# Activation rows of 132 words and longer weight buffers in a two-block transformer kernel

## The chip, the cores and the metric

The kernel runs on one core of one Trainium2 chip. The metric is the device time of one execution in microseconds, as the median of several runs. Engine names: PE is the matrix engine (TensorE), PEld its weight loads, DVE is VectorE, ACT is ScalarE, POOL is GpSimd, SP is SyncE, which issues the transfers.

## What is computed

A residual stream x of 256 tokens by 1024 channels goes through two layers of a first block (feed-forward, a mixer of a linear recurrence, a retention and a short convolution, feed-forward), and then one layer of a second block (two kinds of banded attention, an MLP, a gated embedding). In short:

```
for l in range(2):
    x = x + 0.5 * rmsnorm(swiglu(rmsnorm(x), ffn1_w_in[l], ffn1_w_out[l]))
    x = x + rmsnorm(hybrid_mixer(rmsnorm(x), ...))
    x = x + 0.5 * rmsnorm(swiglu(rmsnorm(x), ffn2_w_in[l], ffn2_w_out[l]))
h = x + rmsnorm(concat(windowed_attention, dilated_attention) @ w_o)
h = h + rmsnorm(relu(rmsnorm(h) @ w_up) ** 2 @ w_down)
out = h + rmsnorm(sigmoid(h @ w_ple_gate + b) * (p @ w_ple_proj))
```

All inputs are float32, and nearly all arithmetic is in products of activations with large weight matrices.

## The kernel before

**Three products for one.** A float32 product is made from three products of a rounded type (`float32r`, four bytes a word). Every activation block and every weight group is split into a rounded part and the rest: `uh`/`ul` for activations, `wh`/`wl` for weights. `mm3` (lines 164 to 171) then issues `uh*wh`, `uh*wl` and `ul*wh` into the same accumulator, on lines 165, 166 and 167. The activation is the stationary operand (128 columns, loaded into the array by a weight load of its own ahead of each matmul), the weight the moving one (512 columns, or 256 in the narrow last chunk of the feed-forward).

**Weights.** 334 groups of 128x2048 words come from memory one after the other. `load` (line 136) takes three tiles: `raw` from a pool of 3 buffers, `wh` and `wl` from a pool with 5 buffers for each name; SP issues the transfer into `raw`. `convert` (line 132) casts `raw` to `wh` on ACT and writes `raw - wh` to `wl` on DVE, in two halves of 1024 words. `grp` (line 153) hands out views of `wh` and `wl`.

**Activations.** `uh[t]` and `ul[t]` (lines 106 and 107), for the two halves t of the tokens, hold the transposed activation as 8 blocks k of 128 words, one block behind the other. They are written by `split` (line 200: a cast on ACT, a subtraction on DVE) in pieces of 4 blocks, after four transposes on PE (`tr_split`, line 235), and read by `proj` (line 270): 8 blocks by 3 products, 24 matmuls, for each 512 output columns of each half. The second kind of product, `acc_out` (line 283), takes its stationary operand from other tiles (`hl`, line 292, out of the pool `b4`, rows of 4096 bytes), four matmul triples to two blocks and two halves of 512 columns.

**Order.** The order of PE's work is that of the program. Other work is put between the triples by `later` (line 172): it counts triples, and what is due is issued by `mm3`; thus four transposes (line 209) stand between matmuls in several places.

**Where the tiles lie.** A tile takes the same range of bytes in each of the 128 partitions, and the pools follow one another: constants, `raw`, `w`, `gain`, `b4`, `b2`, small ones. The sizes are multiples of 128 bytes (`uh0` 4096, `raw` and `wh` 8192, `b4` 4096, `b2` 2048), and the small constants ahead of them are filled up with a tile `even` that nothing reads, so every operand of the `float32r` matmuls starts at a multiple of 128 bytes. Partition memory is nearly full. 16,384 bytes at its start are set aside as scratch for transfers that POOL issues; the kernel issues all its transfers from SP.

Of the kernel before, what the change touches and what calls it, by code (L numbers as in the profile page):

```python
# [12 lines left out]
F32R = mybir.dt.float32r  # L13
# [5 lines left out]
P = 128  # L19
# [53 lines left out]
def build(ctx: ExitStack, tc: tile.TileContext, a: dict, plan: list):  # L73
    nc = tc.nc
    V, A, G, T = nc.vector, nc.scalar, nc.gpsimd, nc.tensor

    def pool(name, bufs, **kw):
        return ctx.enter_context(tc.tile_pool(name=name, bufs=bufs, **kw))

    const = pool("const", 1)  # L80
    rawp = pool("raw", NRAW)
    wp = pool("w", NW)
# [20 lines left out]
    G.memset(mhalf, -0.5)  # L103
    junk = const.tile([P, D], mybir.dt.bfloat16, name="junk")
    x = [const.tile([P, D], F32, name=f"x{t}") for t in range(2)]
    uh = [const.tile([P, 8, P], F32R, name=f"uh{t}") for t in range(2)]
    ul = [const.tile([P, 8, P], F32R, name=f"ul{t}") for t in range(2)]
    cst = const.tile([P, L, 12, 8], F32, name="cst")
    cos = const.tile([P, 2, P], F32, name="cos")
    sin = const.tile([P, 2, P], F32, name="sin")  # L110
# [25 lines left out]
    def load(rec, parts):  # L136
        gi = len(plan)
        plan.append(rec)
        raw = rawp.tile([P, 2048], F32, tag="raw", name=f"raw{gi}")
        wh = wp.tile([P, 2048], F32R, tag="wh", name=f"wh{gi}")  # L140
        wl = wp.tile([P, 2048], F32R, tag="wl", name=f"wl{gi}")
        step = 2048 // parts
        for h in range(0, 2048, step):
            tail[0] = nc.sync.dma_start(raw[:, h:h + step], a["wts"][gi, :, h:h + step])
        return raw, wh, wl
# [7 lines left out]
    def grp(*rec):  # L153
        n = rec[-1]
        if rec in ready:
            raw, wh, wl = ready.pop(rec)
        else:
            raw, wh, wl = load(rec, 1)
            step = 2048 // CONV
            for h in range(0, 2048, step):  # L160
                convert(wh, wl, raw, slice(h, h + step))
        return wh.rearrange("p (k n) -> p k n", n=n), wl.rearrange("p (k n) -> p k n", n=n)
# [771 lines left out]
    for i in range(2):  # L934
        ready[recs[i]] = load(recs[i], 4 - 2 * i)
    nc.sync.dma_start(x[1], a["x"][P:, :])
    for i in range(2, 4):
        ready[recs[i]] = load(recs[i], 1)
# [75 lines left out]
def _layout(inputs):  # L1014
    d = {}
    d["x"] = inputs["x"][0]
    d["positions"] = inputs["positions"].astype(np.int32).reshape(2, P).T
    rows = np.zeros((len(GROW), D), np.float32)
    for (n, l), r in GROW.items():
        if n == "g_out_2":  # L1020
            rows[r] = np.concatenate([inputs["g_out_a_2"][0], inputs["g_out_b_2"][0]])
        else:
            rows[r] = inputs[n][l]
    d["gains"] = rows
    d["g0"] = inputs["ffn1_pre_g"][0].reshape(8, P).T

    def cols(v):
        return v.reshape(L, -1, 8, P).transpose(3, 0, 1, 2)
    d["cst"] = np.concatenate([cols(inputs[n]) for n in (
        "lru_conv_w", "lru_conv_b", "lru_b_a", "lru_b_x", "lru_lambda", "sc_conv_w")]  # L1030
        + [np.zeros((P, L, 1, 8), np.float32)], axis=2)
    w = np.stack([inputs["lru_w_a"], inputs["lru_w_x"]], axis=1).reshape(L, 2, 8, P, 64)
    d["wab"] = w.transpose(0, 3, 1, 2, 4)
    d["rel_bias_table_2"] = inputs["rel_bias_table_2"]
    d["sink_a_2"] = inputs["sink_a_2"]
    d["pT"] = inputs["p_2"][0, 0].T.reshape(2, P, S).transpose(1, 0, 2)
    d.update(_constants())
    return {k: np.ascontiguousarray(v) for k, v in d.items()}


def _weights(inputs, plan):
    w2 = inputs["w_in_2"]
    perm = np.arange(w2.shape[2])
    halves = np.arange(512).reshape(2, 4, 64).transpose(1, 0, 2).reshape(-1)
    for c in (0, 768, 1280):
        perm[c:c + 512] = c + halves
    src = dict(inputs)
    src["w_in_2"] = w2[:, :, perm]
    w = np.empty((NG, P, 2048), np.float32)
    for i, (name, l, k0, kn, c0, n) in enumerate(plan):  # L1050
        blk = src[name][l][k0 * P:(k0 + kn) * P, c0:c0 + n]
        w[i] = blk.reshape(kn, P, n).transpose(1, 0, 2).reshape(P, 2048)
    return w


def _program(inputs):
    import concourse.bacc as _bacc

    nc = _bacc.Bacc("TRN2", target_bir_lowering=False, num_devices=1)
    arrays = _layout(inputs)  # L1060
    args = {n: nc.dram_tensor(n, v.shape, mybir.dt.from_np(v.dtype), kind="ExternalInput").ap()
            for n, v in arrays.items()}
    args["wts"] = nc.dram_tensor("wts", (NG, P, 2048), F32, kind="ExternalInput").ap()
    args["out"] = nc.dram_tensor("out", (S, D), F32, kind="ExternalOutput").ap()
    plan = []
    with tile.TileContext(nc) as tc:
        build(tc, args, plan)
    arrays["wts"] = _weights(inputs, plan)
    return nc, arrays, plan
# [9 lines left out]
```

## Time and profile before

| | before |
|---|---|
| median of three runs | 2024.33 us (2023.94 to 2028.44) |
| the profiled execution, device time | 2028.99 us |
| its span, first to last instruction | 2027.2 us |
| mean granted clock of PE, share of full speed | 0.987 |
| PE busy | 1972.9 us (97%) |
| weight loads busy | 1623.8 us (80%), beside the matmuls |
| DVE busy | 1668.2 us (82%) |
| ACT busy | 1037.3 us (51%) |
| transfers, mean share of the 16 DMA engines | 50% |

The profile is of one execution. Matmuls overlap: one takes some 0.39 us from its start to its end, and the next starts before that end, so the pace of the engine is read from the distances between starts in the timeline, and not from the mean duration. A busy PE is therefore not PE at its peak. Times are read to 0.01 us, so a distance of starts is taken over several matmuls.

### The profile page before, as it was taken

The page shows a single profiled execution, that of the slowest core. Times are in us where ns is not written, and L with a number is a line of the kernel's source. Part 1 is how long each engine was busy: PE and PEld are TensorE (multiplying, and loading weights), DVE is VectorE, ACT ScalarE, POOL GpSimd, SP SyncE. Part 2 cuts the span into 40 slices and gives each one's busy share as a digit, 9 for nine tenths or more (in the row PEclk, how much of TensorE's full clock was granted, in tenths as well). Part 3 has the DMA queues.
Part 4 walks back from the last instruction along what each step waited for, and adds up shares of the span by engine and source line. Part 5 has one row for each costly group of instructions (what it writes and reads, how often), then busy time and mean ns, then how long its engine had stood idle before and what let it go on. Part 6 is the DMA issues. An engine that isn't in the chain of part 4 may idle for free.

```text
span 2027.2 us, 24429 instructions
## 1 busy us (share of the span) xinstructions
PE 1972.9 (97%) x9170; PEld 1623.8 (80%) x9170; DVE 1668.2 (82%) x2893; ACT 1037.3 (51%) x1384; POOL 58.5 (3%) x116
## 2 busy tenths in 40 slices
PE   9999999999999999999999999999999999999997
PEld 7778868788788888888887778887888888787886
DVE  7989789776877998988878995777789897679997
ACT  6444676444444543544466843454454445654553
POOL 0000000000010000000000000000010000010000
PEclk9999999999999999999999999999999999999999
DMA  6555533654445454555653546435545556424542
GB/s 250 192 208 198 187 134 137 244 189 166 166 160 212 173 207 181 198 197 187 239 190 107 183 184 220 169 115 199 205 166 208 198 207 207 161 94 149 220 183 102
DMA packets 56319, 369.72 MB, mean 182 GB/s; under 512 B 6582, under 2 KB 8886, under 8 KB 13704
## 3 DMA queue, kind: packets, MB, share of 16 engines
q1 hardware_dynamic: 56200, 368.16, 49.9%
q8 instruction: 72, 1.18, 0.2%
q14 instruction: 47, 0.39, 0.1%
HBM read 367.05 MB, written 1.08 MB: 182 GB/s over the span
## 4 chain that ended last, share of the span: by engine, by line
PE 65%; DVE 24%; ACT 4%; issue 3%; DMA 2%; POOL 0%; SPq 0%; DVEq 0%; POOLq 0%; ACTq 0%
PE c L165 13%; PE c L166 13%; PE c L167 13%; DVE ht L224 9%; DVE wl L134 8%; PE o L166 7%; PE o L167 7%; PE o L165 7%; DMA raw<-wts 2%; ACT wh L133 2%; DVE sbT L224 2%; DVE ya L224 2%; PE tp L209 2%; PE tp L456 1%; PE pv L762 1%
## 5 line engine op out<-in xcount | busy, mean ns | idle before, releaser
L134 DVE TENSOR_TENSOR wl<-raw,wh 128x1024 fp32r<-128x1024 f32 (+1 forms) x670 | 787.7, 1216 | 171.9 <-ACT wh L133 168.7
L133 ACT CAST wh<-raw 128x1024 fp32r<-128x1024 f32 (+1 forms) x670 | 670.0, 1046 | 336.4 <-PE c L167 163.6
L165 PE MATMUL c<-wh,uh 128*128 128x512 f32 (+1 forms) x1912 | 740.4, 387 | 14.4 <-DVE v L608 5.6
L166 PE MATMUL c<-wl,uh 128*128 128x512 f32 (+1 forms) x1912 | 734.9, 384 | 11.1 <-DVE wl L134 11.1
L167 PE MATMUL c<-wh,ul 128*128 128x512 f32 (+1 forms) x1912 | 734.3, 384 | 0.0
L165 PEld LDWEIGHTS c<-wh,uh 128*128 128x128 f32 x1912 | 363.2, 190 | 89.5 <-DVE v L608 6.5
L166 PEld LDWEIGHTS c<-wl,uh 128*128 128x128 f32 x1912 | 363.4, 190 | 82.5 <-DVE wl L134 12.6
L167 PEld LDWEIGHTS c<-wh,ul 128*128 128x128 f32 x1912 | 362.9, 190 | 71.1 <-issue 1.2
L224 DVE STREAM_TRANSPOSE ht<-sil 32x128 f32<-32x128 f32 (+1 forms) x768 | 223.9, 292 | 10.7
L224 DVE STREAM_TRANSPOSE ht<-sg 32x128 f32<-32x128 f32 x256 | 77.5, 303 | 3.5
L224 DVE STREAM_TRANSPOSE ht<-mh 32x128 f32<-32x128 f32 x256 | 77.5, 303 | 3.4
L195 POOL TENSOR_SCALAR ms<-ss 128x1 f32<-128x1 f32 x52 | 21.9, 421 | 1936.8 <-ACT junk L190 1915.6
L306 ACT ACTIVATE sil<-c,r 128x512 f32<-128x512 f32 (+1 forms) x48 | 31.3, 651 | 41.0 <-PE c L167 40.9
L311 DVE SCALAR_TENSOR_TENSOR sil<-c,r,sil 128x512 f32<-128x512 f32 (+1 forms) x48 | 33.7, 702 | 13.3 <-PE c L167 13.1
L224 DVE STREAM_TRANSPOSE ya<-yat 32x128 f32<-32x128 f32 x128 | 38.7, 302 | 6.0 <-ACT yat L482 4.3
L224 DVE STREAM_TRANSPOSE sbT<-sbt 32x128 f32<-32x128 f32 x128 | 38.8, 303 | 2.0
L197 POOL TENSOR_TENSOR r<-ms,mhalf 128x1 f32<-128x1 f32 x54 | 35.4, 656 | 4.5
L201 ACT CAST h2h<-ht 128x512 fp32r<-128x512 f32 x10 | 6.2, 623 | 52.2 <-DVE ht L224 52.2
L166 PE MATMUL o<-wl,h1h 128*128 128x512 f32 x80 | 31.4, 392 | 0.2 <-DVE wl L134 0.2
L166 PE MATMUL o<-wl,h4h 128*128 128x512 f32 x80 | 31.2, 390 | 0.0
L165 PE MATMUL o<-wh,h3h 128*128 128x512 f32 x80 | 31.2, 390 | 0.0
L166 PE MATMUL o<-wl,h3h 128*128 128x512 f32 x80 | 31.2, 390 | 0.0
(334 smaller groups left out, 2434.1 us busy)
## 6 DMA issues: line engine op xcount, KB each, us to landing
raw<-wts SPq DMA_DIRECT2D x332, 1024.0 KB, 4.8
tb<-row SPq DMA_DIRECT2D x8, 384.0 KB, 5.4
gain_ffn_post_g<-gains SPq DMA_DIRECT2D x4, 512.0 KB, 7.6
dec<-dec SPq DMA_DIRECT2D x4, 384.0 KB, 5.6
gain_ffn_pre_g<-gains SPq DMA_DIRECT2D x3, 512.0 KB, 8.5
x<-x SPq DMA_DIRECT2D x2, 512.0 KB, 5.7
raw<-wts SPq DMA_DIRECT2D x4, 256.0 KB, 5.5
raw<-wts SPq DMA_DIRECT2D x2, 512.0 KB, 6.4
```

The source lines that it names most:

```text
L133: A.copy(wh[:, sl], raw[:, sl])
L134: V.tensor_tensor(wl[:, sl], raw[:, sl], wh[:, sl].bitcast(F32), ALU.subtract)
L165: T.matmul(ps, xh, wh, start=first, stop=False)
L166: T.matmul(ps, xh, wl, start=False, stop=False)
L167: T.matmul(ps, xl, wh, start=False, stop=last)
L195: G.tensor_scalar(ms, ss, mul / n, mul * EPS, ALU.mult, ALU.add)
L197: G.tensor_tensor(r, ms, mhalf, ALU.pow)
L209: T.transpose(tp[:, j, :], src[:, (b + j) * P:(b + j + 1) * P], ident)
L224: V.transpose(dst[32 * j:32 * j + 32, :, 32 * q:32 * q + 32], sv[32 * q:32 * q + 32, :, 32 * j:32 * j + 32])
L306: A.activation(sil[t], ps, AF.Silu, scale=r2[t])
L311: V.scalar_tensor_tensor(sil[t], ps, r2[t], sil[t], ALU.mult, ALU.mult)
L456: T.matmul(ps[b:b + 64, j, :], wab[b:b + 64, g, 4 * c + j0 + j, :], xc[b:b + 64, j0 + j, :], start=True, stop=True)
```

## The change

The blocks of `uh` and `ul` get rows of 132 words of which 128 are used: block k starts 528 k bytes behind the tile's start. Each `wh` and `wl` buffer gets 2056 words of which 2048 are used; `wl` leaves its first 4 words free, so its data start 16 bytes into the buffer. The scratch at the start of partition memory is made smaller, 1024 bytes in place of 16,384. No instruction is added or taken away, and the order is the same.

```diff
-    uh = [const.tile([P, 8, P], F32R, name=f"uh{t}") for t in range(2)]
-    ul = [const.tile([P, 8, P], F32R, name=f"ul{t}") for t in range(2)]
+    uh = [const.tile([P, 8, P + 4], F32R, name=f"uh{t}")[:, :, :P] for t in range(2)]
+    ul = [const.tile([P, 8, P + 4], F32R, name=f"ul{t}")[:, :, :P] for t in range(2)]
...
-        wh = wp.tile([P, 2048], F32R, tag="wh", name=f"wh{gi}")
-        wl = wp.tile([P, 2048], F32R, tag="wl", name=f"wl{gi}")
+        wh = wp.tile([P, 2056], F32R, tag="wh", name=f"wh{gi}")[:, :2048]
+        wl = wp.tile([P, 2056], F32R, tag="wl", name=f"wl{gi}")[:, 4:2052]
...
-    nc = _bacc.Bacc("TRN2", target_bir_lowering=False, num_devices=1)
+    nc = _bacc.Bacc("TRN2", target_bir_lowering=False, num_devices=1, dynamic_dma_scratch_size=1024)
```

What follows for the addresses, as remainders of 128 bytes: `uh` and `ul` tiles are 4224 bytes and start at 0, so block k starts at 16 k. A weight buffer is 8224 bytes, so the five `wh` buffers start at 0, 32, 64, 96 and 0, and the data in the five `wl` buffers at 48, 80, 112, 16 and 48. The ten buffers together are 64 over a multiple of 128, so all that comes behind them (`gain`, `b4`, `b2`) starts at 64: the stationary operands of `acc_out` are all at 64.

## Rows read from the trace of the kernel before

**Rows 1.** The page, part 1: busy us, share of the span, instructions.

```profile
PE 1972.9 (97%) x9170; PEld 1623.8 (80%) x9170; DVE 1668.2 (82%) x2893; ACT 1037.3 (51%) x1384; POOL 58.5 (3%) x116
```

**Rows 2.** Groups by line and shape, PE: busy us, mean ns, idle before and releasers.

```profile
L165 PE MATMUL c<-wh,uh 128*128 128x512 f32 x1752 | 694.9, 397 | 14.4 <-DVE v L608 5.6 <-ACT sil L306 3.5 <-DVE sil L311 3.1
...
L165 PE MATMUL c<-wh,uh 128*128 128x256 f32 x160 | 45.5, 284 | 0.0
...
L165 PE MATMUL o<-wh,h3h 128*128 128x512 f32 x80 | 31.2, 390 | 0.0
```

**Rows 3.** Timeline of PE, a stretch of `acc_out`: start us, duration us, instruction.

```profile
1009.48 0.39 PE L167 MATMUL o<-wh,h3l 128*128 128x512 f32 x1
...
1010.84 0.39 PE L167 MATMUL o<-wh,h3l 128*128 128x512 f32 x1
```

**Rows 4.** Timeline of PE, matmuls of 256 columns.

```profile
999.96 0.28 PE L166 MATMUL c<-wl,uh 128*128 128x256 f32 x1
...
1001.04 0.28 PE L166 MATMUL c<-wl,uh 128*128 128x256 f32 x1
```

**Rows 5.** Timeline of PE in a stretch at the lower clock.

```profile
551.47 0.63 PE L167 MATMUL c<-wh,ul 128*128 128x512 f32 x1
...
554.03 0.63 PE L167 MATMUL c<-wh,ul 128*128 128x512 f32 x1
```

**Rows 6.** Busy us by stretch: length, engines, then granted clock, DMA share, GB/s.

```profile
551.30:554.30 3.00, 3.00 (x8) 2.34 (x8) 3.00 (x4) 2.26 (x3) 0.00 (x0) 0.50 0.82 339
```

**Rows 7.** Timeline of PE behind four transposes.

```profile
225.82 0.39 PE L165 MATMUL c<-wh,uh 128*128 128x512 f32 x1
226.05 0.39 PE L166 MATMUL c<-wl,uh 128*128 128x512 f32 x1
226.28 0.39 PE L167 MATMUL c<-wh,ul 128*128 128x512 f32 x1
226.51 0.60 PE L209 MATMUL tp<-ident,xat 128*128 128x128 f32 x4
226.86 0.48 PE L165 MATMUL c<-wh,uh 128*128 128x512 f32 x1
227.18 0.40 PE L166 MATMUL c<-wl,uh 128*128 128x512 f32 x1
227.41 0.40 PE L167 MATMUL c<-wh,ul 128*128 128x512 f32 x1
227.65 0.40 PE L165 MATMUL c<-wh,uh 128*128 128x512 f32 x1
227.88 0.39 PE L166 MATMUL c<-wl,uh 128*128 128x512 f32 x1
228.10 0.39 PE L167 MATMUL c<-wh,ul 128*128 128x512 f32 x1
...
229.26 0.39 PE L166 MATMUL c<-wl,uh 128*128 128x512 f32 x1
...
229.94 0.39 PE L166 MATMUL c<-wl,uh 128*128 128x512 f32 x1
```

**Rows 8.** What PE waited for, longest first: us, times, longest us.

```profile
PE c L166 <- DVE wl L134: 11.1, 3, 4.0
PE tp L456 <- DVE xc L448: 9.7, 6, 3.2
```

**Rows 9.** Groups of ACT by shape: the cast into `uh`, and one into longer rows.

```profile
L201 ACT CAST uh<-tp 128x512 fp32r<-128x512 f32 x32 | 17.5, 580 | 3.5 <-PE tp L209 3.2
L201 ACT CAST qkh<-tp 128x512 fp32r<-128x512 f32 x16 | 9.3, 581 | 23.3 <-PE tp L209 23.3
```

**Rows 10.** Groups of DVE by shape: the two subtractions.

```profile
L134 DVE TENSOR_TENSOR wl<-raw,wh 128x1024 fp32r<-128x1024 f32 x666 | 785.0, 1219 | 170.5 <-ACT wh L133 167.3
L202 DVE TENSOR_TENSOR ul<-tp,uh 128x512 fp32r<-128x512 f32 x32 | 21.0, 683 | 1.8 <-ACT uh L201 1.5
L202 DVE TENSOR_TENSOR qkl<-tp,qkh 128x512 fp32r<-128x512 f32 x16 | 10.9, 679 | 0.0
```

**Rows 11.** The page, part 3: queues of transfers, packets, MB, share of 16 engines.

```profile
q1 hardware_dynamic: 56200, 368.16, 49.9%
q8 instruction: 72, 1.18, 0.2%
q14 instruction: 47, 0.39, 0.1%
```

## The prediction

> **What bounds the kernel now.** I read the page first. PE is busy 97% of the span and DVE 82% [rows 1], and the waits of PE are small: the largest entry is 11.1 us, the next 9.7 us [rows 8]. So time comes or goes with the pace of PE, and the pace is read from distances between starts.
>
> In a quiet stretch six matmuls of 512 columns take 1010.84 - 1009.48 = 1.36 us, 226.7 ns each [rows 3]. Nine of 256 columns take 1.08 us, 120.0 ns each [rows 4]. At half the granted clock (0.50 [rows 6]) six of 512 columns take 2.56 us, 426.7 ns each [rows 5], which is 512 columns at 1.2 GHz and nothing else. Half of it is 213.3 ns, and that is what 512 columns would take at full clock. So at full clock each matmul pays 13.3 ns on top, and one of 256 columns pays as much (120.0 - 106.7). A cost that is the same for both widths and that vanishes where the columns go by at half the speed is not work of the array; it looks like time lost in bringing operands to it, and a weight load runs beside every matmul. That is the only place where addresses can act on the bound.
>
> How much is at stake: lines 165 to 167 have 3 x 1752 matmuls of 512 columns and 3 x 160 of 256 in the projections [rows 2]. `acc_out` and the small projection of the last block, by the loops of the code, have 840 triples, 2520 matmuls (feed-forwards 352, mixers 320, attention output and MLP 160, embedding 8 triples; one group of 80 is in [rows 2]). Together 8256, and 8256 x 13.3 ns = 110 us, 5.4% of the span. This is the most that the change could give.
>
> **Is the 13.3 ns a matter of phase?** The rows behind four transposes say yes. Before them the distance is 0.23 us. After them the first matmul comes late, and then the distances are 0.23, 0.24, 0.23, 0.22: over the nine matmuls from 227.18 to 229.26 us they make 2.08 us, 231.1 ns each, 4.4 ns over the quiet pace; over the next three, 0.68 us, 226.7 ns again [rows 7]. Nothing has changed in operands, shapes or clock within that stretch; only the time at which the matmuls start has been shifted by the transposes. So the price of a matmul depends on how its stream of words stands in time to something else, and left alone the stream falls back into one stable position, the quiet pace. Two more facts from the same rows: 226.7 and 120.0 ns are 34 and 18 times 6.67 ns, so the quiet paces lie on steps of that size; and among the unquiet distances only one is clearly under the quiet one (0.22 us), most are over it.
>
> All operands of before start at the same remainder of 128 bytes (by the sizes of the tiles), so no row shows two remainders. What they do is bounded from these neighbours.
>
> **The change part by part.**
>
> (a) *Moved operands.* The remainder of the stationary block now moves by 16 bytes from k to k, and the moving operand jumps between `wh` and `wl` at each matmul, between remainders that differ by an odd multiple of 16. If the remainder acts as a shift in time does, the stream is disturbed at each matmul and doesn't come back into the quiet position: it pays the unquiet mean, 4.4 ns more. Projections: 5256 x 4.4 = 23.1 us, and 480 x 4.4 = 2.1 us for the narrow ones. `acc_out`: its stationary operand stays at one remainder (64), but its moving operand alternates as well, 2520 x 4.4 = 11.1 us. Sum 36.3 us. The bounds of a single matmul are the shortest and the longest distance of the stretch, about 0.22 and 0.24 us, so -7 to +13 ns; times 8256 that is -58 to +107 us, and I take the mean of the stretch because the remainders run through many values rather than sit at one.
>
> (b) *Cover.* A slower PE gives DVE and ACT time, and some of PE's waits get shorter; of the 11.1 and 9.7 us [rows 8] I give back 3 us. Net +33 us.
>
> (c) *Splits into `uh` and `ul`.* 32 casts and 32 subtractions (and 4 of each at the start) now write four rows of 128 words with a gap. The nearest rows are those of `qkh` and `qkl`, which write four rows of 128 words 256 apart: 581 against 580 ns, 679 against 683 ns [rows 9, 10]. So 0; bounds of 10 ns either way on 72 instructions are under 1 us, and DVE and PE work beside them.
>
> (d) *`wl` 16 bytes into its buffer.* 666 subtractions of 1219 ns [rows 10]. Subtractions of 512 words differ by some ns between tiles (679 to 683); 13 ns either way would be 9 us of DVE, which has 18% of the span free. I take 0; if the cover were gone, at most the 11.1 us that PE waits for `wl` would grow by a few us.
>
> (e) *Smaller scratch, other base addresses.* The queues are one driven by hardware and two for instructions [rows 11], so nothing uses the scratch: 0. Transfers go into `raw`, whose remainder stays 0.
>
> The sum stands against the profiled execution, 2028.99 us with a span of 2027.2, which is 4.7 us over the median of the runs. The change is taken over to the median: 2024.3 + 33 = 2057.
>
> [...] The rows show a time beside the columns that depends on phase [rows 3 to 5, 7]. [...]
>
> **The rivals.**
>
> *Second road to slower: a line more to read.* The steps of 6.67 ns could be fetches of a piece of fixed size. A stream that starts inside a piece would need one fetch more, one step. If a piece is 64 bytes (512 columns of 4 bytes in 213.3 ns are 64 bytes in 6.67 ns), `wl` always starts inside, `wh` in two buffers of five, so of three matmuls 1 + 2 x 0.4 = 1.8 pay: 0.6 x 6.67 x 8256 = 33 us, 2057 too. Both roads end in the same place, and I count them as one case.
>
> *No change.* If the position in time comes from the instruction stream and not from the operands, remainders do nothing: 2024. For it: the quiet pace is the same whatever buffer and block is read, and whatever ACT and DVE do. Against it: those all share one remainder.
>
> *Faster: starts off the steps.* If the quiet distance is long because every operand starts at the same remainder, each matmul has to wait for the next step of 6.67 ns. With remainders that move, the start may fall anywhere between two steps, and half a step is saved on average: 3.33 x 8256 = 27.5 us, 1997. It decides from the point where the wait for the step is a larger part of the 13.3 ns than the collision with the weight load. For it: both widths lie on whole steps. Against it: behind the transposes the starts are off the steps and the distances are longer, not shorter [rows 7]. In the extreme all 13.3 ns go, 110 us, and then DVE at 1668 us of work would come near to being the bound; I'd put 1940 for that.
>
> *The change doesn't do what it says*: the views are cut from larger tiles, and the addresses follow from sizes; I see no way in which they don't move.
>
> **How the numbers follow.** Slower (unquiet mean or a line more): 0.45, between +15 us (only the projections pay, at half the price) and +45. No change: 0.22. Faster: 0.33, of which 0.22 for about half a step (1990 to 2015) and 0.11 for more. Within 0.3% (6 us) is about what a measurement of this kernel can't tell from no change; this share is nearly all of the no-change case. The predicted time is that of the likeliest case, 2057, whose own range is 2035 to 2070. The range that should hold the time reaches over the no-change case to the mild gain: 1990 to 2070, leaving out 0.10 below and 0.08 above.
>
> **What would show it.** In the changed kernel's timeline, quiet stretches of projections: if their nine-matmul distances are near 231 ns and uneven, (a) holds; if they are even and one step longer in some, the line rival; 226.7 throughout is no change; anything under 224 is the faster rival. In `acc_out` the same should be seen, with two alternating distances. The distances at half clock must stay 426.7 ns. The groups of casts and subtractions must keep their means to 10 ns. The prediction is wrong if remainders act on the collision itself and not only on its timing, since then some remainders could be free of it.

## The result, and the profile after

The change makes the kernel slower: 2043.78 us (2043.75 to 2045.03) against 2024.33, a ratio of 1.0092 with a 95% interval of 1.0069 to 1.0115, or 19.4 us. The forecast was 2057, slower, with 1990 to 2070 as its range. The direction came out, and so did the place of the cost, the pace of PE's matmuls; the reason given for it came out only in part. The size was too large by 13 us, nearly all of it in the step on cover.

The page after, part 1 (busy us, share of the span, instructions); [rows 1] answer to it:

```profile
PE 1998.2 (98%) x9170; PEld 1618.0 (79%) x9170; DVE 1669.2 (82%) x2893; ACT 1037.1 (51%) x1384; POOL 55.8 (3%) x116
```

PE has 25 us more, DVE and ACT the same. Where it comes from is seen in the timeline of PE after (start us, duration us, instruction), in a stretch of a projection and then in one of `acc_out`, which answers [rows 3]:

```profile
752.51 0.39 PE L165 MATMUL c<-wh,uh 128*128 128x512 f32 x1
752.74 0.39 PE L166 MATMUL c<-wl,uh 128*128 128x512 f32 x1
752.97 0.39 PE L167 MATMUL c<-wh,ul 128*128 128x512 f32 x1
753.20 0.40 PE L165 MATMUL c<-wh,uh 128*128 128x512 f32 x1
753.43 0.40 PE L166 MATMUL c<-wl,uh 128*128 128x512 f32 x1
753.67 0.40 PE L167 MATMUL c<-wh,ul 128*128 128x512 f32 x1
...
758.07 0.40 PE L165 MATMUL c<-wh,uh 128*128 128x512 f32 x1
```

```profile
774.78 0.39 PE L165 MATMUL o<-wh,h1h 128*128 128x512 f32 x1
...
780.36 0.39 PE L165 MATMUL o<-wh,h1h 128*128 128x512 f32 x1
```

24 distances of a projection take 5.56 us, 231.7 ns each, and 24 of `acc_out` 5.58 us, 232.5 ns, where before each took 226.7. There are no transposes in either stretch: the quiet pace of before isn't found again in them. Over the whole trace (all distances up to 242 ns between starts of 512-column matmuls outside the stretches at lower clock) the mean goes from 227.1 to 232.0 ns in the projections and from 227.0 to 232.0 in `acc_out`.

The mean granted clock (us from first to last instruction, then the clock), first before, then after:

```profile
core 0: 2027.2 us, clock 0.987
```

```profile
core 0: 2042.0 us, clock 0.994
```

PE ran at the lower of its two levels (0.50, the other is 1.00) for 52.6 us in twelve stretches before and for 24.5 us in six after, by the trace's record of the clock. The waits got shorter too: these two entries answer [rows 8] (us, times, longest us).

```profile
PE c L166 <- DVE wl L134: 8.7, 3, 3.3
PE tp L456 <- DVE xc L448: 7.8, 5, 2.7
```

### The profile page after: what moved, and what is told of

It reads as the page before. It is cut to its first block, busy times and chain, and to the rows that moved or that the text cites. A ratio compares the mean times of both kernels' runs of the same rounds, so it can differ in the third digit from the quotient of the medians.

```text
span 2042.0 us, 24429 instructions
## 1 busy us (share of the span) xinstructions
PE 1998.2 (98%) x9170; PEld 1618.0 (79%) x9170; DVE 1669.2 (82%) x2893; ACT 1037.1 (51%) x1384; POOL 55.8 (3%) x116
## 3 DMA queue, kind: packets, MB, share of 16 engines
q8 instruction: 72, 1.18, 0.2%
## 4 chain that ended last, share of the span: by engine, by line
PE 74%; DVE 18%; ACT 3%; DMA 2%; issue 2%; POOL 0%; SPq 0%; DVEq 0%; POOLq 0%; ACTq 0%
PE c L165 16%; PE c L166 16%; PE c L167 16%; PE o L165 7%; PE o L167 7%; PE o L166 7%; DVE ht L224 6%; DVE wl L134 5%; DMA raw<-wts 2%; DVE sbT L224 2%; PE tp L209 2%; DVE ya L224 2%; ACT wh L133 1%; PE tp L456 1%; PE pv L762 1%
## 5 line engine op out<-in xcount | busy, mean ns | idle before, releaser
L311 DVE SCALAR_TENSOR_TENSOR sil<-c,r,sil 128x512 f32<-128x512 f32 (+1 forms) x48 | 33.7, 702 | 14.4 <-PE c L167 14.2
L165 PE MATMUL o<-wh,h4h 128*128 128x512 f32 x80 | 31.6, 396 | 0.0
L165 PE MATMUL o<-wh,h2h 128*128 128x512 f32 x80 | 31.6, 395 | 0.0
```

The source lines that it names most:

```text
L165: T.matmul(ps, xh, wh, start=first, stop=False)
L311: V.scalar_tensor_tensor(sil[t], ps, r2[t], sil[t], ALU.mult, ALU.mult)
```

## The experiments

The changed kernel does three things at once: smaller scratch, longer rows of the stationary operand, longer buffers of the moving one. Runs 1 to 4 take them apart, runs 6 to 8, 10 and 11 go through constant differences, and runs 5, 9 and 12 settle what kind of remainder counts. All have three rounds against the kernel before on the same chip. A difference means: remainder of the stationary operand less that of the moving one, for the weight load that runs beside a matmul. Paces are distances of starts between 512-column matmuls; a mean over the trace is taken as above. Remainders and differences are worked out from the sizes of the tiles and the order of the pools.

**Theory and rivals at the start.** A: each move of a remainder disturbs the phase, and the quiet position is lost. B: a moving operand that starts inside a piece of 64 bytes costs a step. Later C, D, E as the expectations say.

**1. The scratch alone.**

```diff
-    nc = _bacc.Bacc("TRN2", target_bir_lowering=False, num_devices=1)
+    nc = _bacc.Bacc("TRN2", target_bir_lowering=False, num_devices=1, dynamic_dma_scratch_size=1024)
```

> The kernel before with the smaller scratch alone, so that all tiles move down by 15,360 bytes and every matmul operand keeps the remainder 0 of 128 bytes. Every theory of remainders: no change, 2024 us, and quiet stretches at 226.7 ns from start to start for 512 columns. If the place in memory matters by more than its remainder, or the scratch is used, something else; then the 19.4 us of the change are not those of its remainders.

Measured: ratio 1.0003 (0.9993 to 1.0012), projections 227.1 ns, `acc_out` 226.9, clock 0.986. The scratch doesn't count, and neither does moving every tile by 15,360 bytes, which keeps all remainders up to 512. All kernels below have this edit too.

**2. Longer rows of the stationary operand alone.**

```diff
-    uh = [const.tile([P, 8, P], F32R, name=f"uh{t}") for t in range(2)]
+    uh = [const.tile([P, 8, 132], F32R, name=f"uh{t}")[:, :, :P] for t in range(2)]
```

(The same for `ul`, here and in all runs below that change `uh`.)

> The scratch and the rows of 132 words in uh and ul; weight buffers as before. Only the stationary operand of the projections moves through remainders, the moving one stays at 0 everywhere. Theory A (a disturbed phase: any stream whose remainder moves from matmul to matmul loses the quiet position): projections at about 231 ns mean and uneven, acc_out quiet at 226.7; +5256 x 4.5 = 24 us gross, less what the waits and the low clock give back, so 2035 to 2045. Theory B (a moving operand that starts inside a piece of 64 bytes costs one step more): no moving operand is off, so no change, 2024.

Measured: 2038.1 us, ratio 1.0053 (1.0037 to 1.0069). The timeline of this kernel, a projection and a stretch of `acc_out`:

```profile
749.52 0.39 PE L165 MATMUL c<-wh,uh 128*128 128x512 f32 x1
...
755.07 0.40 PE L165 MATMUL c<-wh,uh 128*128 128x512 f32 x1
```

```profile
738.64 0.39 PE L165 MATMUL o<-wh,h0h 128*128 128x512 f32 x1
...
744.08 0.39 PE L165 MATMUL o<-wh,h0h 128*128 128x512 f32 x1
```

24 distances: 231.3 ns in the projection, 226.7 in `acc_out`. The cost sits exactly where the remainder of the stationary operand moves, and the moving operand, which theory B makes pay, was never touched. B falls here.

**3. Longer weight buffers alone.**

```diff
-        wh = wp.tile([P, 2048], F32R, tag="wh", name=f"wh{gi}")
-        wl = wp.tile([P, 2048], F32R, tag="wl", name=f"wl{gi}")
+        wh = wp.tile([P, 2056], F32R, tag="wh", name=f"wh{gi}")[:, 0:2048]
+        wl = wp.tile([P, 2056], F32R, tag="wl", name=f"wl{gi}")[:, 4:2052]
```

> The scratch and the longer weight buffers; uh and ul as before. Moving operands take changing remainders in all products, stationary ones stay at 0 in the projections and at 64 in acc_out. Theory A: both kinds at about 231 ns, uneven, 2035 to 2045, about as slow as the whole change. Theory B: nearly the whole cost, with distances that are whole steps (226.7 or 233.3) and go by the buffer: matmuls whose moving operand starts at 0 or 64 stay at 226.7.

Measured: 2045.5 us, ratio 1.0084 (1.0067 to 1.0100); means of 231.7 ns in the projections and 232.0 in `acc_out`, uneven. A projection takes 5.58 us for 24 distances, 232.5 ns:

```profile
752.37 0.40 PE L165 MATMUL c<-wh,uh 128*128 128x512 f32 x1
...
757.95 0.39 PE L165 MATMUL c<-wh,uh 128*128 128x512 f32 x1
```

Moving the moving operand is enough for the whole cost, and adding the rows (the changed kernel) costs nothing more. The two edits don't add: in runs 2 and 3 and in the changed kernel the pace is either the quiet one or some 5 ns over it.

**4. All moving operands at 16.**

```diff
+        wh = wp.tile([P, 2080], F32R, tag="wh", name=f"wh{gi}")[:, 4:2052]
+        wl = wp.tile([P, 2080], F32R, tag="wl", name=f"wl{gi}")[:, 4:2052]
```

> The scratch, and all weight data, wh and wl, at 16 bytes behind a multiple of 128; stationary operands stay at 0. So all remainders are constant again, but moving and stationary ones differ, in all products. Theory A: a quiet position exists again and the even pace is back, a whole number of steps of 6.67 ns: 226.7 (2024 us) or one step beside it (220.0, 1970 us, or 233.3, 2078 us). Theory B: each of 8256 matmuls of 512 and 256 columns pays one step, 55 us, 2079 us, even. A price by the difference of the two remainders alone (a collision): even, and at another pace than 226.7.

Measured: 2036.6 us, ratio 1.0046 (1.0030 to 1.0063); 230.0 ns in the projections and 230.1 in `acc_out`, not even but in short repeating groups such as 234, 234, 225 ns. Here 24 distances of a projection take 5.52 us, 230.0 ns:

```profile
750.09 0.40 PE L165 MATMUL c<-wh,uh 128*128 128x512 f32 x1
...
755.61 0.40 PE L165 MATMUL c<-wh,uh 128*128 128x512 f32 x1
```

Theory A as it was put expected an even pace back, and B 55 us more; neither came. The run was less clean than its text says: a buffer of 8320 bytes keeps the remainder of 128 and not that of 256, which alternates from buffer to buffer. So by 256 bytes the difference still moves (112 and 240), and whether a constant one pays is left to runs 6 to 11.

**5. Rows of 160 words: remainder 0 of 128.**

```diff
+    uh = [const.tile([P, 8, 160], F32R, name=f"uh{t}")[:, :, :P] for t in range(2)]
```

> The scratch and rows of 160 words in uh and ul: block k starts 640 k bytes behind the tile's start, again a multiple of 128, with the same four-row writes as with 132 words. All theories that go by the remainder of 128 bytes: no change, 2024 to 2028 us, projections even at 226.7 ns. If the gap, the longer rows or the shape of the writes made the cost, it stays: 2035 us or more.

Measured: 2038.2 us, ratio 1.0050 (1.0035 to 1.0065). A miss for everything that went by 128 bytes:

```profile
749.56 0.39 PE L165 MATMUL c<-wh,uh 128*128 128x512 f32 x1
...
755.13 0.40 PE L165 MATMUL c<-wh,uh 128*128 128x512 f32 x1
```

232.1 ns over 24 distances. So either a larger modulus counts or the gap between the rows does.

**6 to 8. Constant differences.** Stationary operands of `acc_out` are shifted as a whole by a tile between the pools; `uh` and `ul` by words at the start of a longer tile. For 16 and 32 bytes:

```diff
+    padp = pool("pad", 1)
     gp = pool("g", NGN)
...
+    padp.tile([P, 8], F32, name="padw")
...
+    uh = [const.tile([P, 1056], F32R, name=f"uh{t}")[:, 4:1028].rearrange("p (k n) -> p k n", n=P) for t in range(2)]
```

> Moving operands all at 0. Stationary ones at a constant remainder: 16 in the projections, 32 in acc_out. The run before this one with a constant difference (moving at 16, stationary at 0) lost the even pace: 234, 234, 225 ns in turn, 231.1 mean. Theory C (the price goes by the difference of the two remainders and the phase together; only some differences have an even pace): two paces, one for each kind of product, each between 224 and 234 ns, 2025 to 2050 us. Theory D (a collision of the two reads of the array at equal remainders): differences far from 0 are free of it, 216 to 220 ns, 1960 to 1990 us. Theory B (pieces of 64 bytes, moving operand alone): no change.

> As the run with 16 and 32, with 48 in the projections and 64 in acc_out. Theory C: two paces between 224 and 234 ns. Theory D: if the two reads collide at equal remainders, 64 is farthest from it, and acc_out falls to 216 to 220 ns, 2520 x 8 ns = 20 us less there.

> As the run with 16 and 32, with 80 in the projections and 96 in acc_out; with the run with moving operands at 16 (difference 112) and the kernel before (difference 0) all eight differences of 16 bytes are then measured. Theory C: two paces between 224 and 234 ns. Theory D: under 222 ns in both.

Measured: ratios 1.0090 (1.0075 to 1.0105), 1.0083 (1.0068 to 1.0098) and 1.0087 (1.0070 to 1.0104). `acc_out`, with all remainders constant, ran at 233.2 ns for 32, 233.3 for 64 and 234.1 for 96. The projections (232.4, 231.6, 232.0) mix two differences, since tiles of 4224 bytes shift the remainder of 256 by 128 from one half of the tokens to the other; within a projection of one half the difference is constant. Taken by halves, the means are 232.2 ns for 16 and 232.5 for 144 (run 6), 233.1 for 48 and 230.1 for 176 (run 7), 232.0 for 80 and 232.1 for 208 (run 8). The best of them, 176, in run 7, 20 distances in 4.60 us, 230.0 ns:

```profile
423.61 0.39 PE L168 MATMUL c<-wl,uh 128*128 128x512 f32 x1
...
428.21 0.39 PE L167 MATMUL c<-wh,uh 128*128 128x512 f32 x1
```

No mean is under the quiet pace, so D finds no free difference; and a remainder that never moves costs as much as one that does. Theory A falls: movement is not needed for the cost.

Run 6 shows one thing more, at one and the same difference. These are two projections of the same half (difference 16) at the full granted clock, and the matmul between them that waited for DVE:

```profile
904.99 0.39 PE L167 MATMUL c<-wh,uh 128*128 128x512 f32 x1
...
909.75 0.39 PE L167 MATMUL c<-wh,uh 128*128 128x512 f32 x1
...
910.95 0.50 PE L167 MATMUL c<-wh,uh 128*128 128x512 f32 x1 [0.36 <-DVE sil L313]
...
916.66 0.40 PE L167 MATMUL c<-wh,uh 128*128 128x512 f32 x1
...
921.56 0.40 PE L167 MATMUL c<-wh,uh 128*128 128x512 f32 x1
```

21 distances take 4.76 us ahead of the wait, 226.7 ns each, and 4.90 us behind it, 233.3 ns. Of 197 such stretches of 15 or more distances in this run's projections (16 or 144), 28 settle at 226.7 ns and 169 at 233.3, none between (by the mean of their last twelve distances). Where one stretch follows the other with nothing in between, the pace stays (105 times of 105); at each of the 19 changes something came in between, such as a wait or transposes. So at these two differences the phase decides as well, as theory C had it ("the difference of the two remainders and the phase together").

**9. Rows of 192 words: remainder 0 of 256.**

```diff
+    uh = [const.tile([P, 8, 192], F32R, name=f"uh{t}")[:, :, :P] for t in range(2)]
```

> The scratch and rows of 192 words in uh and ul: block k starts 768 k bytes behind the tile's start, so remainders of 128 are all 0, of 256 all 0, and of 512 they alternate between 0 and 256. Rows of 160 words (remainder 0 of 128, alternating 0 and 128 of 256) cost as much as rows of 132, against what every theory of 128 bytes said. Theory E (what counts is the difference of the two remainders of 256 bytes): no change, 2024 to 2028 us, projections even at 226.7 ns. Theory F (512 bytes, or the gap and the shape of the writes): 2035 to 2042 us, as with 160 and 132 words.

Measured: ratio 0.9996 (0.9985 to 1.0007).

```profile
746.45 0.39 PE L165 MATMUL c<-wh,uh 128*128 128x512 f32 x1
...
751.89 0.39 PE L165 MATMUL c<-wh,uh 128*128 128x512 f32 x1
```

226.7 ns again, with a gap in the rows too and remainders of 512 that alternate. Against run 5 the gap is 128 bytes longer and the remainder of 256 is constant; run 10, which has no gap and pays at a difference of 128, leaves the remainder of 256 as the one that counts.

**10 and 11. The remaining constant differences.** As run 6, with tiles of 1152 words, so that all remainders of 512 are constant, and shifts of 32 and 48 words, then 56 and 40.

> Moving operands at 0 and stationary ones at a constant remainder of 512 bytes: 128 in the projections, 192 in acc_out. Theory E: the difference 0 is the best of all and others have paces of 228 to 235 ns, so 2040 to 2050 us. Theory D in what is left of it (some difference is free of the collision, and with a modulus of 256 bytes the farthest is 128): projections at 216 to 222 ns, 2024 - 5256 x 6 = 1990 us or less.

> As the run with 128 and 192, with 224 in the projections and 160 in acc_out. With the runs before, differences of 0, 32, 64, 96, 160 and 192 are then measured in acc_out and 128, 224 in the projections, each with all remainders constant. Theory E: 228 to 235 ns in both, 2040 to 2050 us. Theory D: one of them under 222 ns.

Measured: ratios 1.0085 (1.0070 to 1.0100) and 1.0111 (1.0096 to 1.0126). The timeline of run 10, a projection (difference 128) and `acc_out` (192):

```profile
756.27 0.39 PE L167 MATMUL c<-wh,uh 128*128 128x512 f32 x1
756.50 0.40 PE L168 MATMUL c<-wl,uh 128*128 128x512 f32 x1
756.73 0.39 PE L169 MATMUL c<-wh,ul 128*128 128x512 f32 x1
756.96 0.40 PE L167 MATMUL c<-wh,uh 128*128 128x512 f32 x1
757.20 0.39 PE L168 MATMUL c<-wl,uh 128*128 128x512 f32 x1
...
761.87 0.39 PE L167 MATMUL c<-wh,uh 128*128 128x512 f32 x1
```

```profile
745.27 0.39 PE L167 MATMUL o<-wh,h0h 128*128 128x512 f32 x1
...
750.77 0.39 PE L167 MATMUL o<-wh,h0h 128*128 128x512 f32 x1
```

24 distances take 5.60 us (233.3 ns) and 5.50 us (229.2 ns). In run 11 a projection (difference 224) takes 5.60 us for 24, 233.3 ns:

```profile
755.40 0.40 PE L167 MATMUL c<-wh,uh 128*128 128x512 f32 x1
...
761.00 0.39 PE L167 MATMUL c<-wh,uh 128*128 128x512 f32 x1
```

No difference is free, so D falls. Run 11 costs no less than the changed kernel (ratio 1.0092, 1.0069 to 1.0115) although nothing in it moves, and both kinds of product are at 233.3 ns where the changed kernel has 232.0.

**12. Everything at 64.** Moving and stationary operands all at remainder 64, by the same means (weight tiles of 2176 words, data 16 words in).

> Every matmul operand, moving and stationary, at remainder 64: the addresses are no longer whole multiples of 128, but the difference is 0. Theory E (the difference alone counts): even again at 226.7 ns, no change, 2024 to 2028 us. Theory B (a start inside a piece costs one step, or aligned starts are what makes the quiet pace): disturbed or a step more, 2040 us or more.

Measured: ratio 0.9988 (0.9979 to 0.9998).

```profile
746.60 0.39 PE L167 MATMUL c<-wh,uh 128*128 128x512 f32 x1
...
752.04 0.39 PE L167 MATMUL c<-wh,uh 128*128 128x512 f32 x1
```

226.7 ns. At the difference 0 the address itself doesn't count (64 is the one tried). What theory E said of its four runs came out, run 11 at the edge (2050.1 us where it had 2040 to 2050). Run 6 limits it: at 16 and 144 the difference alone doesn't settle the pace.

The constant differences together, as means over the whole trace; first those where all remainders of 256 are constant in a product, then those that are constant within a projection of one half:

| difference, bytes of 256 | 0 | 32 | 64 | 96 | 128 | 160 | 192 | 224 |
|---|---|---|---|---|---|---|---|---|
| ns from start to start | 227.0 | 233.2 | 233.3 | 234.1 | 232.7 | 233.3 | 229.1 | 233.3 |
| taken from | before, `acc_out` | run 6, `acc_out` | run 7, `acc_out` | run 8, `acc_out` | run 10, projections | run 11, `acc_out` | run 10, `acc_out` | run 11, projections |

| difference, bytes of 256 | 16 | 48 | 80 | 144 | 176 | 208 |
|---|---|---|---|---|---|---|
| ns from start to start | 232.2 | 233.1 | 232.0 | 232.5 | 230.1 | 232.1 |
| taken from (projections) | run 6 | run 7 | run 8 | run 6 | run 7 | run 8 |

The kernel before has the best of these fourteen differences in every product. 112 and 240 were seen only mixed with others (run 4, 230.1).

## Why the prediction was right, and where it was off

**Step (a), moved operands: the size held, its reason only in part.** The forecast took 4.4 ns for every matmul from the stretch behind four transposes [rows 7]. Measured: 4.9 ns in the projections, 5.0 in `acc_out`; 5256 x 4.9 + 2520 x 5.0 = 38 us where the sum had 23.1 + 11.1 = 34.2. The transposes shift the start of the stream in time and the remainder shifts it in address, and both ended near the same mean. That the two agree so well is in part luck: single constant differences cost from 2.1 ns (192) to 7.1 ns (96). And the step said that the stream pays *because the remainders run through many values*. Runs 10 and 11 hold them constant and pay as much, run 9 moves them by 256 and pays nothing. What is lost is the difference 0 of 256 bytes, the only one of those measured that comes back to the even pace of 226.7 ns after the disturbances: in the kernel before, all 94 stretches of 15 or more distances (as taken for the means) end at it, with 226 or 227 ns in at least five of the last six. So the quiet position behind the transposes isn't a property of any undisturbed stream, as the prediction took it; it is sure at the difference 0, was reached in 28 of 197 stretches at 16 and 144, and was seen at none of the other eleven.

**The narrow matmuls** were to cost 2.1 us more and gave a little back. After, ten distances of 256 columns take 1.18 us, 118 ns, where [rows 4] have 120.0:

```profile
1007.32 0.28 PE L166 MATMUL c<-wl,uh 128*128 128x256 f32 x1
...
1008.50 0.28 PE L167 MATMUL c<-wh,ul 128*128 128x256 f32 x1
```

Over the trace the mean goes from 120.4 to 118.8 ns, 480 x 1.6 = 0.8 us. Why these win where the wide ones lose is open.

**Step (b), cover: the term that was mis-sized.** The prediction gave back 3 us. In the profiled executions the matmuls cost 38 - 0.8 = 37 us more and the span only 14.8 (2042.0 - 2027.2), so 22 us were given back. Two entries account for it, the waits and the clock. The waits that are put down to lines 165, 166 and the lru products, which [rows 2, 8] show at 14.4, 11.1 and 9.7 us, fell to 8.1, 8.7 and 7.8, 10.6 us in all; that a slower PE lets DVE and ACT catch up is the author's reading of it. The first of the three, after:

```profile
L165 PE MATMUL c<-wh,uh 128*128 128x512 f32 x1752 | 700.2, 400 | 8.1 <-DVE v L608 4.1 <-ACT sil L306 2.7 <-DVE sil L311 0.7
```

And the clock: (1 - 0.987) x 2027.2 = 26.4 us were lost to the lower level before, (1 - 0.994) x 2042.0 = 12.3 us after, up to 14 us less (part of these stretches are waits, so the two entries overlap). An estimate without the overlap: 80 of the matmuls of lines 165 to 167 start at the lower level before and 34 after, each some 0.2 us longer ([rows 5] against [rows 3]), 16 us and 7 us, so the clock gave back 9 us there. The prediction had read the lower clock only as a lens on the 13.3 ns [rows 5, 6], and not as a cost that shrinks when PE gets slower. (Its 1.2 GHz are 512 columns over the 426.7 ns; the trace has the clock as a share only, 0.50.) The runs bear the pattern out: in the profiled executions the three even kernels, runs 1, 9 and 12, have a clock of 0.986, the nine disturbed ones 0.990 to 0.995. That it is the shorter waits that keep the clock up is argued from this and was not tried by itself. The medians differ by 19.4 us rather than 14.8, because the profiled execution of before was 4.7 us over its median. That median is of three executions; in the rounds of the experiments the kernel before has medians of 2027.6 to 2028.2 us over 7 to 19. Against these the cost would be about 16 us, an estimate, since the changed kernel has no run in those rounds; the 33 us of the forecast are then 17 us too large rather than 13.

**Steps (c), (d), (e)** held. The cast into `uh` and the subtractions, after, against [rows 9, 10]:

```profile
L201 ACT CAST uh<-tp 128x512 fp32r<-128x512 f32 x32 | 17.7, 580 | 3.7 <-PE tp L209 3.6
```

```profile
L134 DVE TENSOR_TENSOR wl<-raw,wh 128x1024 fp32r<-128x1024 f32 x666 | 785.2, 1220 | 182.6 <-ACT wh L133 179.7
L202 DVE TENSOR_TENSOR ul<-tp,uh 128x512 fp32r<-128x512 f32 x32 | 21.0, 684 | 3.2 <-ACT uh L201 2.9
```

580, 1220 and 684 ns against 580, 1219 and 683: writing four rows with a gap, or 16 bytes into a buffer, costs nothing that can be measured. Run 1 shows that the scratch costs nothing.

**The rivals.** *A line more to read* named the same time and was counted with the forecast; run 2 refutes it, with the whole moving side untouched and the projections slow. *No change* falls with the paces. *Faster, off the steps* falls with the tables: no difference gives starts that come sooner on the mean, and the row that spoke against it, the longer distances behind the transposes, was the right one to trust. The pace is not free of where the stationary operand lies against the moving one: runs 9, 10 and 12 issue the same instructions on the same data, and it is 226.7 ns at the difference 0 (runs 9 and 12) and 233.3 ns at 128 (run 10, projections). What is lost between the two operands, no run shows.

## What to carry to other kernels

When PE is the bound, measure the distance between starts in a quiet stretch and just behind a disturbance: here they differed (226.7 and 231.1 ns, [rows 3, 7]), and edits that moved the operands against each other cost up to 7 ns a matmul, where moving all tiles alike cost nothing (run 1). For four-byte `float32r` operands with a new weight load for every matmul, keep stationary and moving operands at the same remainder of 256 bytes; here a padding tile or another row length cost 2 to 7 ns on each matmul of 512 columns (229.1 to 234.1 ns against 227.0 in the tables), and the profile showed it in the distances between starts and in PE's busy time (1998.2 against 1972.9 us in the changed kernel), but in no wait. The cost added to the bounding engine was not paid in full here: some 22 of 37 us came back, with shorter waits (10.6 us) and less time at the lower clock (24.5 us for 52.6), so price both before summing.

## What the hardware showed that was not expected

What counted is the remainder of 256 bytes, not of 128: run 5 (232.1 ns) against run 9 (226.7), and run 10 (233.3 at 128). At the difference 0 the pace was the same at both addresses tried: 226.7 ns at 0 [rows 3] and at 64 (run 12). At 16 and 144 the same operands run at either of two paces, 226.7 and 233.3 ns, and the pace changed only where the stream was interrupted: run 6 (19 changes, and none in 105 stretches that follow another with nothing in between).

In the stretches shown the distances settle into a short pattern whose sum is a whole number of steps of 6.67 ns: 226.7 (34 steps) for 0; 229 and 238 in turn for 128 (70 steps, run 10); 226, 229 and 232 for 192 (103 steps, run 10); 231, 235, 233 and 234 for 224 (140 steps, run 11); 236, 229, 226 and 229 for 176 (138 steps, run 7). The 233.3 ns that many differences come to are 35 steps, one more than the quiet pace, on the mean and not matmul by matmul. In the kernel before, all 115 stretches of eight or more matmuls with distances of 226 or 227 ns start at the same place within a step, to 0.2 ns over the 2 ms, once a drift of 1.5 ns per ms is taken off. So in this trace the starts of the quiet stretches keep to one beat of 6.67 ns. What it is, and why the pace repeats after a single matmul always at 0 and only sometimes at 16 and 144, stays open; so do the differences 112 and 240 by themselves, and the 13.3 ns, which no kernel here brought down (an estimate: the 226.7 ns of [rows 3] less the 213.3 of 512 columns at the 106.7 that the 256 columns more take against [rows 4]).
